# ConvFFN in three chunks of features, w_down by seven block products instead of eight, and pool tiles that wait only for the users of their own bytes

## The chip, the cores and the metric

The kernel runs as one program on one core of one Trainium2 chip. The metric is the device time of that core in microseconds (us); lower is better. A profiled execution of the same program gives the trace from which rows are read below. Engines are named as in the profile: PE is the matrix engine (PEld its weight loads), DVE the vector engine, ACT the scalar engine, POOL GpSimd, SP the engine that issues most DMAs. SBUF is the on-chip memory of 128 partitions; PSUM is the memory into which PE accumulates.

## The reference

One trunk layer is computed for 128 context tokens and 512 latent tokens (640 columns in all). The first part (adaptive norm, latent attention, a bidirectional state-space scan, gates, output projection) leaves a residual stream x of 1024 features. The change rewrites the last part, the ConvFFN:

```python
h2 = rmsnorm(x, lp['norm_ffn_g']) * (1 + sc2) + sh2
u = dwconv_centred(h2 @ lp['w_up'], lp['ffn_conv_w'], lp['ffn_conv_b'])
x = x + g2 * ((jax.nn.silu(u[..., :D_FF]) * u[..., D_FF:]) @ lp['w_down'])
y = rmsnorm(x, final_norm_g)
```

D_FF is 2816, so `w_up` is 1024 x 5632 and `w_down` 2816 x 1024. `dwconv_centred` is a depthwise convolution of width 3 along the tokens, for each request by itself.

## The kernel before

Data stand with features on partitions and the 640 tokens along the free axis; a tile of 128 features x 640 tokens is a "page" (2.5 KB a partition, 21 of them in the pool `pg`). Every matmul of weights is done to nearly full fp32 precision with three passes of the fp32r type: an operand is split into a high part (an ACT cast, L105) and a low part (a subtraction on POOL or DVE, L102), and `mm3` (L129) multiplies high by high, high by low and low by high. One 128 x 128 block of weights against 640 tokens is therefore six matmuls, three of 384 columns and three of 256 (`halves`), each with its own weight load.

Weights come by `wload`: an SP DMA into `raw` (4 buffers of 1024 columns), an ACT cast into `whi`, a POOL subtraction into `wlo` (2 buffers each), all in the pool `ws`, which lives through the whole kernel. So a whole tile of weights can be fetched and split while the tile before it is multiplied.

The ConvFFN follows the output projection. While the last three output tiles are finished, `h2_part` (L1142) makes the eight pages of h2 for the first 384 tokens and then for the other 256; it reads and overwrites the tiles `x1` of the pool `hold`. One `w_up` tile (`early`) and the first tiles of the loop run in between. Then 22 feature tiles are made (L1184): for each, two products with h2 into PSUM `big` (2 buffers), `conv` (ACT L453, four DVE instructions L455 and L458), SiLU (L1200), a multiply (L1201), and the split into the high and low part, 22 pairs of pages kept in `fl`, `fr` and `pg`. After that (L1209) each of the eight output tiles m runs over all 22 feature tiles, is added to x (`residual`, L1094) and squared for the last norm; the last tile does its two token parts one after the other, so that the norm and the output of the first (L1248) run beside the products of the second.

PE, ACT, DVE and POOL each execute their own list of instructions in order. Inside `tc.manual_schedule(engines=...)` the lists of the named engines are in the order of the program text; elsewhere a planner orders by its own estimates, the earlier in the text first among those that are ready. SP's DMAs are one such list too, so a DMA that waits for its buffer holds those behind it.

Tile pools are regions of SBUF that are opened and closed like a stack. Inside a pool each tag has its buffers in a row, tags in order of first use. When a pool is opened over the bytes of closed ones, its tiles wait for all users of those pools. The pools whose opening the prediction speaks of: `sp` (for the scan, L837, over `op2`, `sm` and `ar` of the attention's output), `yp` (L1043, over `sd` and `sp`), `hold` (L1106), `fl` and `fr` (L1181).

Of the kernel before, what the change touches and what calls it, by code (L numbers as in the profile page):

```python
# [10 lines left out]
F32 = mybir.dt.float32  # L11
F32R = mybir.dt.float32r
AF = mybir.ActivationFunctionType
ALU = mybir.AluOpType
# [45 lines left out]
RP = 2  # L60
LAG, F_T, F_V = 2, (1, 2), (1, 0, 1, 1, 1)
# [10 lines left out]
def trunk_kernel(ctx: ExitStack, tc: tile.TileContext, a: dict):  # L72
# [51 lines left out]
    def mm3(outs, hi, lo, rhs, first, last):  # L124

        plan = [(hi, rhs[0]), (hi, rhs[1]), (lo, rhs[0])]
        for i, (w, r) in enumerate(plan):
            for o, s in outs:
                PE.matmul(o, w, r[:, s], start=first and i == 0, stop=last and i == 2)  # L129
# [134 lines left out]
    tmp = sqp.enter_context(tc.tile_pool(name="tmp", bufs=3))  # L264
# [33 lines left out]
    gp = sqp.enter_context(tc.tile_pool(name="gp", bufs=16))  # L298
# [192 lines left out]
    op = ost.enter_context(tc.tile_pool(name="op", bufs=8, side="right"))  # L491
    awk = ExitStack()
    ap = awk.enter_context(tc.tile_pool(name="ap", bufs=1))
# [231 lines left out]
    sd = swk.enter_context(tc.tile_pool(name="sd", bufs=1))  # L725
    op2 = att.enter_context(tc.tile_pool(name="op2", bufs=16))
# [6 lines left out]
    xp = xst.enter_context(tc.tile_pool(name="xp", bufs=8, side="right"))  # L733

    sm = att.enter_context(tc.tile_pool(name="sm", bufs=1))
# [74 lines left out]
    ar = att.enter_context(tc.tile_pool(name="ar", bufs=1))  # L810
# [26 lines left out]
    sp = swk.enter_context(tc.tile_pool(name="sp", bufs=1))  # L837
# [205 lines left out]
    yp = ssd.enter_context(tc.tile_pool(name="yp", bufs=16))  # L1043
# [19 lines left out]
    mp = mst.enter_context(tc.tile_pool(name="mp", bufs=16, side="right"))  # L1063
    mer = []
    sxs = ExitStack()
    sx = sxs.enter_context(tc.tile_pool(name="sx", bufs=1, side="right"))
# [39 lines left out]
    hp_ = hold.enter_context(tc.tile_pool(name="hold", bufs=1))  # L1106
# [71 lines left out]

    sxs.close()
    mst.close()  # L1180
    fl = ctx.enter_context(tc.tile_pool(name="fl", bufs=28))  # L1181
    fr = ctx.enter_context(tc.tile_pool(name="fr", bufs=14, side="right"))
    act = []
    for i in range(NF):  # L1184
        us = []
        for j in range(2):
            if i == 1 and j == 0:
                p = early
# [20 lines left out]
    for m in range(8):  # L1209
# [5 lines left out]
        for k0 in range(0, NF, step):  # L1215
# [3 lines left out]
            if not last:  # L1219
                if k0 == 0:  # L1220
                    ps = big()
# [165 lines left out]
```

## Time and profile before

| what | us |
|---|---|
| median of three runs (1280.89 to 1287.76) | 1281.18 |
| the profiled execution, its own time | 1281.07 |
| its span in the trace | 1279.3 |
| PE busy within the span | 1217.2 |
| DVE, ACT, POOL busy | 727.4, 542.9, 496.7 |
| from the first products of the 22 feature tiles to the end | about 482 (797 to 1279) |

The busy time of PE counts overlapping matmuls once; it says that PE had work in flight, and only the number of matmuls in a stretch tells the pace. Of the other engines' times one reads whether they leave room beside PE in a given stage.

### The profile page before, as it was taken

How to read it: one execution, taken by the hardware profiler on the slowest of the kernel's cores; microseconds unless marked ns; L12 is line 12 of the kernel's file. 1: busy time of each engine (PE TensorE's matmuls, PEld its weight loads, DVE VectorE, ACT ScalarE, POOL GpSimd, SP SyncE). 2: the span in 40 equal slices, each digit the busy share in tenths (PEclk: the TensorE clock that was granted, in tenths of full speed). 3: DMA queues.
4: the chain of work that ended last, by engine and by line, in shares of the span. 5: the costliest groups of instructions: out<-in, count | busy, mean ns of one | idle time of the engine just before them, and what ended most of it. 6: DMA issues, size and time to landing. Idle time of an engine off the chain costs nothing. (4 is left out here: it accounts for less than half of the span.)

```text
span 1279.3 us, 20744 instructions
## 1 busy us (share of the span) xinstructions
PE 1217.2 (95%) x8361; PEld 1165.6 (91%) x8361; DVE 727.4 (57%) x1285; ACT 542.9 (42%) x943; POOL 496.7 (39%) x260
## 2 busy tenths in 40 slices
PE   8798999999998989899988998999999999999997
PEld 5698999999998987788888898999999999999996
DVE  4767656665558876866779989644444434300003
ACT  5455455545557425534763232533333333311220
POOL 3433021211213328845567365333333323334450
PEclk9999999999998999899989899999999999999999
DMA  8333221213128762123365674122212122242212
GB/s 330 127 102 102 80 68 54 80 68 108 54 95 284 250 230 93 63 81 108 103 219 186 219 246 133 42 82 67 82 67 83 67 82 68 84 151 75 75 46 83
DMA packets 53680, 148.23 MB, mean 116 GB/s; under 512 B 6224, under 2 KB 11792, under 8 KB 53584
## 3 DMA queue, kind: packets, MB, share of 16 engines
q1 hardware_dynamic: 51824, 144.80, 33.5%
q10 hardware_dynamic: 1760, 2.11, 0.6%
q8 instruction: 66, 1.08, 0.4%
q14 instruction: 30, 0.25, 0.1%
HBM read 124.01 MB, written 20.35 MB: 113 GB/s over the span
## 5 line engine op out<-in xcount | busy, mean ns | idle before, releaser
L129 PE MATMUL big<-pg,whi 128*128 128x384 f32 (+1 forms) x3752 | 726.8, 314 | 6.7 <-DVE pg L1083 4.4
L129 PEld LDWEIGHTS big<-pg,whi 128*128 128x128 f32 x3752 | 572.8, 190 | 19.9 <-issue 11.6
L102 POOL TENSOR_TENSOR wlo<-raw,whi 128x1024 fp32r<-128x1024 f32 (+1 forms) x128 | 319.8, 2499 | 593.0 <-ACT whi L105 587.4
L129 PE MATMUL big<-pg,wlo 128*128 128x384 f32 (+1 forms) x1876 | 436.6, 312 | 6.1 <-POOL wlo L102 6.0
L129 PEld LDWEIGHTS big<-pg,wlo 128*128 128x128 f32 x1876 | 292.5, 191 | 7.7 <-POOL wlo L102 7.1
L105 ACT CAST whi<-raw 128x1024 fp32r<-128x1024 f32 (+2 forms) x133 | 135.1, 1017 | 187.5 <-PE big L129 169.4
L455 DVE SCALAR_TENSOR_TENSOR st<-big,vec,st 128x127 f32<-128x127 f32 x68 | 37.0, 544 | 104.9 <-ACT st L453 104.9
L1094 DVE SCALAR_TENSOR_TENSOR pg<-big,mod,pg 128x128 f32<-128x128 f32 (+2 forms) x15 | 7.5, 542 | 124.8 <-PE big L129 124.8
L105 ACT CAST pg<-pg 128x640 fp32r<-128x640 f32 x46 | 33.0, 727 | 105.0 <-DVE pg L1201 67.1
L129 PE MATMUL sm<-pg,whi 128*128 128x384 f32 (+1 forms) x256 | 63.1, 327 | 4.1 <-ACT pg L105 2.5
L102 DVE TENSOR_TENSOR pg<-pg,pg 128x640 fp32r<-128x640 f32 x43 | 41.1, 963 | 23.8 <-ACT pg L105 23.8
L250 DVE SCALAR_TENSOR_TENSOR araw<-araw,crow 128x1024 f32<-128x1024 f32 x32 | 52.6, 1644 | 0.5
L129 PEld LDWEIGHTS sm<-pg,whi 128*128 128x128 f32 x256 | 46.0, 197 | 7.2 <-ACT pg L105 2.8
L455 DVE SCALAR_TENSOR_TENSOR pg<-big,vec,pg 128x127 f32<-128x127 f32 (+1 forms) x42 | 22.9, 546 | 51.3 <-ACT pg L453 51.3
L102 DVE TENSOR_TENSOR ptl<-sm,pth 128x512 fp32r<-128x512 f32 (+1 forms) x48 | 29.6, 620 | 35.0 <-ACT pth L600 35.0
L584 ACT ACTIVATE p<-sm,st 128x320 f32<-128x320 f32 x64 | 33.2, 524 | 37.6 <-DVE st L582 37.6
L581 DVE TENSOR_REDUCE st<-sm 128x1 f32<-128x320 f32 (+1 forms) x72 | 31.5, 462 | 26.5 <-PE sm L577 26.5
L250 DVE SCALAR_TENSOR_TENSOR junk<-araw,crow 128x1024 f32<-128x1024 f32 x32 | 45.7, 1428 | 0.0
L600 ACT CAST pth<-sm 128x512 fp32r<-128x512 f32 (+1 forms) x48 | 25.5, 533 | 43.7 <-PE sm L597 43.5
L129 PE MATMUL sm<-pg,wlo 128*128 128x384 f32 (+1 forms) x128 | 41.3, 323 | 0.3 <-POOL wlo L102 0.3
L458 DVE SCALAR_TENSOR_TENSOR st<-big,vec,st 128x127 f32<-128x127 f32 x68 | 37.2, 547 | 1.7
L1200 ACT ACTIVATE pg<-pg 128x640 f32<-128x640 f32 x22 | 16.3, 739 | 47.6 <-DVE pg L458 47.6
(294 smaller groups left out, 1737.3 us busy)
## 6 DMA issues: line engine op xcount, KB each, us to landing
raw<-w_up SPq DMA_DIRECT2D x44, 512.0 KB, 3.2
araw<-w_adar SPq DMA_DIRECT2D x32, 512.0 KB, 4.9
araw<-w_ada SPq DMA_DIRECT2D x16, 512.0 KB, 7.8
raw<-w_down SPq DMA_DIRECT2D x14, 512.0 KB, 3.5
raw<-w_xbc SPq DMA_DIRECT2D x12, 512.0 KB, 3.3
raw<-w_gm SPq DMA_DIRECT2D x8, 512.0 KB, 3.2
raw<-w_o_mla SPq DMA_DIRECT2D x8, 512.0 KB, 3.2
raw<-w_z SPq DMA_DIRECT2D x8, 512.0 KB, 4.5
```

Of the source, the lines that this page charges most:

```text
L102: return eng.tensor_tensor(out, x, f(hi), ALU.subtract)
L105: ACT.copy(hi, src)
L129: PE.matmul(o, w, r[:, s], start=first and i == 0, stop=last and i == 2)
L250: DVE.scalar_tensor_tensor(out, raw, 1.0, crow[r], ALU.mult, ALU.mult, accum_out=mod[:, j, r : r + 1])
L455: DVE.scalar_tensor_tensor(dst[:, lo_ + 1 : hi_], p[:, lo_ : hi_ - 1], vec[:, w : w + 1], dst[:, lo_ + 1 : hi_], ALU.mult, ALU.add)
L458: DVE.scalar_tensor_tensor(dst[:, lo_ : hi_ - 1], p[:, lo_ + 1 : hi_], vec[:, w + 2 : w + 3], dst[:, lo_ : hi_ - 1], ALU.mult, ALU.add)
L581: DVE.reduce_max(st[:, i : i + 1], sv, AX.X)
L584: ACT.activation(p[:, i * w : (i + 1) * w], sv, AF.Exp, bias=st[:, 2:3], scale=SCALE, accum_out=st[:, 4 + i : 5 + i])
L600: return ph, pl, ACT.copy(ph[:, :n], pt[:, :n]), sub(DVE, pl[:, :n], pt[:, :n], ph[:, :n])
L1094: ins = DVE.scalar_tensor_tensor(dst[:, lo_:hi_], ps[:, lo_ - cols.start : hi_ - cols.start], mod[:, gcol, r : r + 1], src[:, lo_:hi_], AL ...
L1200: ACT.activation(us[0], us[0], AF.Silu)
```

## The change

**Pools.** All pools but the constants, the pages, `ws` and PSUM get `reuse_waits="tile"`: a tile of such a pool waits for the users of the bytes that it covers, no longer for those of whole closed pools. `ws` is opened above `pg` and closed before the ConvFFN, where new pools `wf`, `kp` and `xs` take its place and that of the pools above it.

**Chunks.** The 22 feature tiles are worked in three chunks, 0 to 7, 8 to 15 and 16 to 21. After a chunk's tiles are made, their share of `w_down` is applied to all eight output tiles and added to x, which goes to DRAM and back between chunks.

**Seven products.** Within a chunk, feature tiles are taken in pairs (top, bottom), output tiles in pairs, and the tokens in two halves of 320, which makes a 2 x 2 by 2 x 2 block product. `blocks` makes the sums of activations that a seven-product scheme needs, `Pair.add` those of the weights, `Pair.product` runs the seven products with accumulation in three PSUM regions (`pa`, `pb`, `pc`), and `Pair.out` combines them into x on DVE. Weights are split in blocks of 512 columns (`operand`, tags `sh` and `sl`, 8 buffers each) rather than 1024. Between the chunks the two products of the next feature tile are run first. In the last chunk output tiles 0 to 3 are done so; 4 to 7 are done plainly, the first 384 tokens before and between the pairs, the other 256 after them.

The diff, cut to its core:

```diff
+CHUNKS = (0, 8, 16)
+LEAD, ON_DVE = 5, (4, 6)
...
-    ws = ctx.enter_context(tc.tile_pool(name="ws", bufs=2))
     pg = ctx.enter_context(tc.tile_pool(name="pg", bufs=21))
+    wss = ctx.enter_context(ExitStack())
+    ws = wss.enter_context(tc.tile_pool(name="ws", bufs=2))
...
-    sp = swk.enter_context(tc.tile_pool(name="sp", bufs=1))
+    sp = swk.enter_context(tc.tile_pool(name="sp", bufs=1, reuse_waits="tile"))
...
+    wss.close()
+    N2 = T // 2
+    lft, rgt = slice(0, N2), slice(N2, T)
+    ws = ctx.enter_context(tc.tile_pool(name="wf", bufs=2, reuse_waits="tile"))
+    kp = ctx.enter_context(tc.tile_pool(name="kp", bufs=24, reuse_waits="tile"))
+    xq = ctx.enter_context(tc.tile_pool(name="xs", bufs=4, reuse_waits="tile"))
...
+    def operand(x, n, eng):
+        hi, lo = (ws.tile([128, 512], F32R, tag=t, name=nm(t), bufs=8) for t in ("sh", "sl"))
+        h_, l_ = hi[:, 0:n], lo[:, 0:n]
+        if len(x.shape) == 3:
+            h_, l_ = (t.rearrange("p (i c) -> p i c", c=128) for t in (h_, l_))
+        split(h_, l_, x, eng)
+        return hi, lo
...
+    def blocks(i, top, bot):
+        ta = page()
+        DVE.tensor_tensor(ta[:, lft], top[:, rgt], top[:, lft], ALU.subtract)
+        DVE.tensor_tensor(ta[:, rgt], bot[:, rgt], ta[:, lft], ALU.subtract)
+        if i >= CHUNKS[-1]:
+            if i < NF - 1:
+                t = page(F32R, kp)
+                b12[i] = (t[:, lft], t[:, rgt])
+            else:
+                b12[i] = (half(), half())
+            split(*b12[i], top[:, rgt])
+        DVE.tensor_tensor(top[:, rgt], bot[:, rgt], top[:, rgt], ALU.subtract)
+        out = []
+        for t in (top, bot, ta):
+            out.append((page(F32R, kp), page(F32R, kp)))
+            split(*out[-1], t)
+        DVE.tensor_tensor(bot[:, rgt], bot[:, lft], ta[:, rgt], ALU.subtract)
+        out.append((half(), half()))
+        split(*out[-1], bot[:, rgt])
+        ops[i] = out
...
+    class Pair:
...
+        def add(self, n):
+            s = self.sums
+            x, y, op = {
+                1: lambda: (self.a21, self.a22, ALU.add),
+                2: lambda: (s[1], self.a11, ALU.subtract),
+                3: lambda: (self.a11, self.a21, ALU.subtract),
+                4: lambda: (self.a12, s[2], ALU.subtract),
+            }[n]()
+            s[n] = ws.tile([128, 512], F32, tag="sum", name=nm("sum"), bufs=4)[:, 0 : self.n * 128].rearrange("p (i c) -> p i c", c=128)
+            DVE.tensor_tensor(s[n], x, y, op)
+        def put(self, n):
+            s = self.sums
+            x = (lambda: self.a11, lambda: s[2], lambda: s[3], lambda: s[1], lambda: self.a12, lambda: s[4], lambda: self.a22)[n]()
+            self.w.append(operand(x, self.n * 128, DVE if n in ON_DVE else POOL))
+        def product(self, n):
+            if n == 0:
+                if self.last:
+                    self.pa, self.pb, self.pc, self.t = bank
+                else:
+                    ab = big()
+                    self.pa, self.pb, self.pc = ab[:, 0:N2], ab[:, 512 : 512 + N2], small()[:, 0:N2]
+            ps, b, cols, on = (
+                (self.pa, 0, lft, False), (self.pb, 2, rgt, False), (self.pc, 0, rgt, False), (self.pb, 2, lft, True),
+                (self.pa, 1, lft, True), (self.pb, 1, rgt, True), (self.pc, 3, lft, True),
+            )[n]
+            hi, lo = self.w[n]
+            for k in range(self.n):
+                s = slice(k * 128, (k + 1) * 128)
+                mm3([(ps, cols)], hi[:, s], lo[:, s], ops[self.k0 + 2 * k + 1][b], not on and k == 0, k == self.n - 1, on)
+        def temp(self):
+            return self.t if self.last else small()[:, 0:N2]
+        def to_x(self, j, ps, cols):
+            residual(self.x[j], ps, 40 + self.m + j, self.x[j], cols)
+        def out(self, n):
+            if n == 0:
+                self.p1 = part()
+                ACT.copy(self.p1, self.pa)
+            elif n == 1:
+                self.u2 = part()
+                DVE.tensor_tensor(self.u2, self.pb, self.p1, ALU.add)
+            elif n == 3:
+                u4, t = part(), self.temp()
+                DVE.tensor_tensor(u4, self.pb, self.p1, ALU.add)
+                DVE.tensor_tensor(t, self.pc, u4, ALU.add)
+                self.to_x(1, t, rgt)
+            elif n == 4:
+                self.to_x(0, self.pa, lft)
+            elif n == 5:
+                t = self.temp()
+                DVE.tensor_tensor(t, self.pb, self.p1, ALU.add)
+                self.to_x(0, t, rgt)
+            elif n == 6:
+                t = self.temp()
+                DVE.tensor_tensor(t, self.pc, self.u2, ALU.add)
+                self.to_x(1, t, lft)
+                if not self.last:
+                    for j in range(2):
+                        nc.sync.dma_start(xcd[self.c][self.m + j], self.x[j])
+    xcd = [[tc.dram_tile([128, T], F32, name=f"scr_xc{c}_{m}") for m in range(8)] for c in range(len(CHUNKS) - 1)]
+    def pairs(new, behind=(), between=None):
+        for t in range(7 * len(new) + 1):
+            g, s = divmod(t, 7)
+            if t:
+                new[(t - 1) // 7].out((t - 1) % 7)
+            if g == len(new):
+                break
+            now, nxt = new[g], new[g + 1] if g + 1 < len(new) else None
+            if s == 2:
+                if nxt:
+                    nxt.load_x()
+                if g + 2 < len(new):
+                    new[g + 2].load()
+            if nxt:
+                for n in ((1,), (2,), (), (3,), (), (4,), ())[s]:
+                    nxt.add(n)
+            n = s + LEAD - 7
+            if between and t == 7:
+                between()
+            if n < 0:
+                now.put(n + 7)
+            elif nxt:
+                if between and n == 0:
+                    behind[0]()
+                nxt.put(n)
+            elif n < len(behind) and not between:
+                behind[n]()
+            now.product(s)
...
+    made = {}
+    for c in range(len(CHUNKS) - 1):
+        first, nxt = CHUNKS[c], CHUNKS[c + 1]
+        for i in range(first + (c > 0), nxt):
+            for j in range(2):
+                u = made.pop((i, j), None) or Up(i, j)
+                if (i, j) != (1, 0):
+                    u.fetch()
+                if (i, j) == (nxt - 1, 1):
+                    ahead = [Up(nxt, 0), Up(nxt, 1)]
+                    for v in ahead:
+                        v.fetch()
+                    new = [Pair(c, m) for m in range(0, 8, 2)]
+                    new[0].load()
+                    ready(new[0])
+                    for n in range(LEAD - 1):
+                        new[0].put(n)
+                up_tile(u, early if (i, j) == (1, 0) else None)
+        with tc.manual_schedule(engines={PE.engine, ACT.engine, DVE.engine, POOL.engine}):
+            us[nxt, 0] = up_conv(nxt, 0, ahead[0].product())
+            silu(us[nxt, 0])
+            new[0].put(LEAD - 1)
+            new[0].load_x()
+            new[1].load()
+            us[nxt, 1] = up_conv(nxt, 1, ahead[1].product())
+            DVE.tensor_tensor(us[nxt, 0], us[nxt, 0], us.pop((nxt, 1)), ALU.mult)
+            nu = [Up(nxt + 1, j) for j in range(2)]
+            made = {(nxt + 1, j): nu[j] for j in range(2)}
+            behind = [lambda: (nu[0].load(), nu[0].put(0)), lambda: nu[0].put(1), lambda: (nu[1].load(), nu[1].put(0)), lambda: nu[1].put(1)]
+            pairs(new, behind)
...
+            if (i, j) == (NF - 1, 0):
+                new = [Pair(c, m) for m in (0, 2)]
+                new[0].load()
+                ready(new[0])
+                for n in range(LEAD):
+                    new[0].put(n)
...
+    def cut(i, c):
+        top, bot, *_ = ops[i | 1]
+        if i % 2:
+            return [(bot, c, slice(0, c.stop - c.start))]
+        out = []
+        if c.start < N2:
+            n = min(c.stop, N2) - c.start
+            out.append((top, slice(c.start, c.start + n), slice(0, n)))
+        if c.stop > N2:
+            s = max(c.start, N2)
+            out.append((b12[i | 1], slice(s - N2, c.stop - N2), slice(s - c.start, c.stop - c.start)))
+        return out
+    def plain(m, ps, c, ks):
+        for k in ks:
+            if k < NF - 1:
+                s = slice((k - k0) * 128, (k - k0 + 1) * 128)
+                w = wn[m]
+                s = slice((m - 4) * 128, (m - 3) * 128)
+                w = wlast
+            cs_ = cut(k, c)
+            plan = [(w[0], 0), (w[0], 1), (w[1], 0)]
+            for n, (w_, x) in enumerate(plan):
+                for b, src, o in cs_:
+                    PE.matmul(
+                        ps[:, o], w_[:, s], b[x][:, src], start=k == k0 + 1 and n == 0, stop=k == ks[-1] and n == 2,
+                        skip_group_check=True,
+                    )
...
+    ks = [k0 + 1, k0, *range(k0 + 2, NF)]
+    c0, c1 = PARTS
+    whole = slice(0, T)
+    with tc.manual_schedule(engines={PE.engine, ACT.engine, DVE.engine, POOL.engine}):
+        pn = [small()[:, 0:HALF] for _ in tiles]
+        for m, ps in zip(tiles, pn):
+            plain(m, ps, c0, ks[:-1])
+        ab, cd = big(), big()
+        bank = (ab[:, 0:N2], ab[:, 512 : 512 + N2], cd[:, 0:N2], cd[:, 512 : 512 + N2])
+        raw = rawtile()[:, 0:512]
+        nc.sync.dma_start(
+            raw.rearrange("p (m c) -> p m c", c=128), a["w_down"][4:8, :, (NF - 1) * 128 : NF * 128].rearrange("m p c -> p m c")
+        )
+        wlast = []
+        new[0].load_x()
+        new[1].load()
+        for m in tiles:
+            x2[m] = page()
+            nc.sync.dma_start(x2[m], xcd[-1][m])
+        def between():
+            x2[0], x2[1] = new[0].x
+            for m in (0, 1):
+                finished(m, whole, whole)
+            for m, ps in zip(tiles, pn):
+                plain(m, ps, c0, ks[-1:])
+                residual(x2[m], ps, 40 + m, x2[m], c0)
+                finished(m, c0, c0)
+            sqrt_table(acc)
+        pairs(new, [lambda: wlast.extend(operand(raw, 512, POOL))], between)
+        x2[2], x2[3] = new[1].x
+        for m in (2, 3):
+            finished(m, whole, c1)
+        last = [sqs[2], sqs[3]]
+    def scaled_out(rp, c):
         for m in range(8):
             g = vec[:, V_GFIN + m : V_GFIN + m + 1]
             DVE.scalar_tensor_tensor(x2[m][:, c], x2[m][:, c], g, rp, ALU.mult, ALU.mult)
             nc.sync.dma_start(a["out_y"][m][:, c], x2[m][:, c])
+    with tc.manual_schedule(engines={PE.engine}):
+        w1 = c1.stop - c1.start
+        ab, cd = big(), big()
+        for m, ps in zip(tiles, (ab[:, 0:w1], ab[:, 512 : 512 + w1], cd[:, 0:w1], cd[:, 512 : 512 + w1])):
+            plain(m, ps, c1, ks)
+            if m == 5:
+                ss = sumsq([acc, *last], c0)
+            if m == 6:
+                scaled_out(rstd_rows(ss, D, c0), c0)
+            residual(x2[m], ps, 40 + m, x2[m], c1)
+            finished(m, c1, c1 if m < 7 else None)
+        scaled_out(rstd_rows(sumsq([acc, sqs[7]], c1), D, c1), c1)
```

## Rows read from the trace of the kernel before

**Rows 1.** Page of the profile, its first line.

```profile
span 1279.3 us, 20744 instructions
```

**Rows 2.** Chain of work that ended last: start, time, engine, line.

```profile
822.16 425.27 PE big L129 x2892
```

**Rows 3.** Windows, the stretch of `w_down`: busy of PE, PEld, DVE, ACT, POOL; clock.

```profile
1010.00:1247.00 237.00, 237.00 (x1613) 237.00 (x1612) 50.88 (x88) 65.86 (x78) 92.03 (x44) 1.00 0.27 83
```

**Rows 4.** Timeline of PE, 128-column matmuls: start, busy time.

```profile
331.30 0.28 PE L129 MATMUL sm<-kh,ql 128*128 128x128 f32 x1
331.41 0.27 PE L577 MATMUL sm<-krh,qr 128*128 128x128 f32 x1
331.52 0.27 PE L577 MATMUL sm<-krl,qr 128*128 128x128 f32 x1
```

**Rows 5.** Timeline of DVE near 810, splitting `x1`.

```profile
809.70 0.42 DVE L102 TENSOR_TENSOR pg<-x,pg 128x256 fp32r<-128x256 f32 x1
```

**Rows 6.** Groups by form of PE, 797 to 811.4, matmuls of `big`.

```profile
L129 PE MATMUL big<-pg,whi 128*128 128x384 f32 x30 | 8.8, 349 | 0.0
L129 PE MATMUL big<-pg,wlo 128*128 128x384 f32 x14 | 4.7, 336 | 0.0
```

**Rows 7.** Windows, 811.4 to 822.16, columns as before.

```profile
811.40:822.16 10.76, 9.40 (x70) 8.62 (x70) 6.94 (x18) 6.31 (x11) 4.95 (x5) 1.00 0.01 2
```

**Rows 8.** Timeline, one feature tile from conv to split.

```profile
1097.69 0.88 ACT L453 ACTIVATE st<-big,vec 128x640 f32<-128x640 f32 x1
...
1100.82 0.82 DVE L1201 TENSOR_TENSOR pg<-pg,st 128x640 f32<-128x640 f32 x1
...
1101.67 0.73 ACT L105 CAST pg<-pg 128x640 fp32r<-128x640 f32 x1 [3.10 <-DVE pg L1201]
```

**Rows 9.** Groups by form of DVE, whole run: count, busy, mean ns.

```profile
L998 DVE TENSOR_TENSOR k<-k,k 128x512 f32<-128x512 f32 x20 | 28.5, 1424 | 12.4 <-POOL k L997 10.3 <-ACT k L988 2.1
...
L1010 DVE TENSOR_TENSOR k<-sm,pg 128x512 f32<-128x512 f32 x16 | 10.3, 683 | 1.2 <-PE sm L1008 1.2
...
L102 DVE TENSOR_TENSOR ql<-sm,qh 128x320 fp32r<-128x320 f32 x16 | 7.1, 484 | 9.5 <-ACT qh L105 9.5
L1094 DVE SCALAR_TENSOR_TENSOR x<-sm,mod,x 128x256 f32<-128x256 f32 x14 | 6.7, 476 | 1.6 <-PE sm L129 1.6
...
L1094 DVE SCALAR_TENSOR_TENSOR x<-sm,mod,x 128x128 f32<-128x128 f32 x8 | 2.8, 344 | 3.3 <-PE sm L129 3.3
```

**Rows 10.** Groups by form of ACT, whole run.

```profile
L105 ACT CAST qh<-sm 128x320 fp32r<-128x320 f32 x16 | 6.0, 429 | 3.4 <-PE sm L129 3.4
...
L1200 ACT ACT_TABLE_LOAD x1 | 1.3, 1283 | 0.0
```

**Rows 11.** Timeline of PE, its longest wait there in brackets.

```profile
410.12 0.72 PE L767 MATMUL sm<-dA,cons 128*128 128x80 f32 x2 [5.53 <-DVE dA L764]
```

**Rows 12.** Windows behind two waits, clock in the column after POOL.

```profile
410.00:414.00 4.00, 3.88 (x16) 3.88 (x17) 4.00 (x9) 2.45 (x4) 0.00 (x0) 0.54 0.74 242
478.50:482.00 3.50, 3.50 (x17) 3.50 (x16) 1.51 (x3) 2.70 (x6) 1.46 (x2) 0.51 1.01 316
```

**Rows 13.** Timeline of DVE, the scaled output near the end.

```profile
1263.94 4.29 DVE L1248 SCALAR_TENSOR_TENSOR pg<-pg,vec,sm 128x384 f32<-128x384 f32 x8 [1.01 <-PE sm L175]
```

**Rows 14.** Timeline around the loads of `bc`; SPq issues DMAs.

```profile
471.94 0.23 DVE L251 TENSOR_SCALAR mod<-mod,vec 128x2 f32<-128x2 f32 x1
471.98 1.75 SPq L846 DMA_DIRECT2D bc<-scr_xbc  x4
...
476.28 0.33 PE L857 MATMUL sm<-cons,bc 128*128 128x128 f32 x1 [0.54 <-ACT bc L847]
...
478.16 0.33 PE L857 MATMUL sm<-cons,bc 128*128 128x128 f32 x1 [1.55 <-ACT bc L847]
```

**Rows 15.** Timeline of DVE, one of the products for `ys`.

```profile
654.30 0.87 DVE L1056 SCALAR_TENSOR_TENSOR pg<-pg,vec,pg 128x640 fp32r<-128x640 f32 x1
```

**Rows 16.** Groups by form of POOL, 822 to 1010.

```profile
L102 POOL TENSOR_TENSOR wlo<-raw,whi 128x1024 fp32r<-128x1024 f32 x27 | 64.7, 2397 | 122.8 <-ACT whi L105 122.8
```

More of the change, by code (lines that the diff above doesn't have):

```diff
@@ L128, in mm3 @@
             for o, s in outs:
-                PE.matmul(o, w, r[:, s], start=first and i == 0, stop=last and i == 2)
+                PE.matmul(o, w, r[:, s], start=first and i == 0, stop=last and i == 2, skip_group_check=on)
     def halves(ps):
@@ new lines, in operand, with __init__, load, fetch @@
+    def operand(x, n, eng):
[5 more added lines that the diff above has]
+        return hi, lo
+    class Up:
+        def __init__(self, i, j):
+            self.i, self.j, self.w = i, j, []
+        def load(self):
+            self.raw = rawtile()
+            nc.sync.dma_start(self.raw, a["w_up"][2 * self.i + self.j])
+        def put(self, n):
+            self.w.append(operand(self.raw[:, 512 * n : 512 * n + 512], 512, POOL))
+        def fetch(self):
+            if not self.w:
+                self.load()
+                self.put(0)
+                self.put(1)
+        def product(self):
+            ps = big()
+            for outs in [[o] for o in halves(ps)] if self.i == 0 else [halves(ps)]:
+                for k in range(8):
+                    (hi, lo), s = self.w[k // 4], slice(k % 4 * 128, k % 4 * 128 + 128)
+                    mm3(outs, hi[:, s], lo[:, s], h2[k], k == 0, k == 7)
+            return mid(ps)
@@ new lines, in ready, with up_tile, up_join @@
+    def ready(pair):
+        for n in (1, 2, 3, 4):
+            pair.add(n)
+    us = {}
+    def up_tile(u, p=None):
+        i, j = u.i, u.j
+        if p is None:
+            u.fetch()
+            p = u.product()
+        us[i, j] = up_conv(i, j, p)
+        if j:
+            up_join(i)
+            if i % 2:
+                blocks(i, us.pop((i - 1, 0)), us.pop((i, 0)))
+    def up_join(i):
+        silu(us[i, 0])
+        DVE.tensor_tensor(us[i, 0], us[i, 0], us.pop((i, 1)), ALU.mult)
@@ new lines, in trunk_kernel @@
+    c = len(CHUNKS) - 1
+    k0 = CHUNKS[c]
+    nk = NF - k0
+    tiles = range(4, 8)
+    wn = {}
+    for i in range(k0 + 1, NF):
+        for j in range(2):
+            up_tile(made.pop((i, j), None) or Up(i, j))
+            if i == NF - 2:
+                for m in tiles[2 * j : 2 * j + 2]:
+                    raw = rawtile()[:, 0 : (nk - 1) * 128]
+                    nc.sync.dma_start(raw, a["w_down"][m][:, k0 * 128 : (NF - 1) * 128])
+                    hi, lo = ((page(F32R, xq if j else kp)) for _ in range(2))
+                    split(hi, lo, raw, POOL)
+                    wn[m] = (hi, lo)
+            if (i, j) == (NF - 1, 0):
[4 more added lines that the diff above has]
+                    new[0].put(n)
```

131 lines of the change are left out of this document (56 added, 75 removed).

## Prediction

> **What bounds the kernel now.** I read the page's head first for the span: 1279.3 us of the execution's 1281.07, so 1.8 us lie around it [rows 1]. Then the chain of work that ended last: its longest step is matmuls of `mm3` alone, from 822.16 for 425.27 us [rows 2]. Then windows for the pace inside it: while `w_down` runs, PE is busy all 237.00 us with 1613 matmuls, 0.1469 us each [rows 3]. They are half of 384 and half of 256 columns, 320 in the mean, so columns set the time: 0.46 us per 1000 columns, or 0.175 for 384, 0.1175 for 256 and 0.147 for 320. Matmuls of 128 columns start 0.11 us apart, where columns alone would give 0.06 [rows 4]; short ones have a floor. The reader is to see that here only fewer columns or fewer waits of PE count; DVE, ACT and POOL are busy 51, 66 and 92 of 237 us in it. Ahead of 797 PE has its waits, and there the pools' edges matter.
>
> **The change part by part**, against 1281.07.
>
> *Columns of `w_down`.* Before: 8 x 22 x 6 = 1056 matmuls x 0.1469 = 155.1 us. After, products by seven: 2 chunks x 4 pairs x 7 x 4 x 3 = 672, and 2 pairs x 7 x 3 x 3 = 126, so 798 x 0.147 = 117.3. The four plain tiles need each 9 x 0.175 for odd features, 9 x (0.147 + 0.11) for even ones, whose 384 columns come as 320 + 64, and 18 x 0.1175: 6.0, in all 24.0. Sum 141.3: **-13.8**. The 36 pieces of 64 columns are bounded by the floor (taken, since 128 columns stand there already) and by their columns (0.03), which makes -16.7.
> The Trainium skill ("TensorE: Matmul & The Clock Gate", section "LDWEIGHTS (loading the stationary operand)") has the weight load take time by the columns of the weights, 107 ns for 128, however few columns then stream through; the rows agree (0.11). By it the pieces cost an estimated 2.8 us above their columns; if loads hid behind the neighbour, the sum would be 2.9 lower.
>
> *Start of the ConvFFN.* The new pool `wf` lies where `ws` and the pools above it were: `raw` on its old bytes, the high parts on `whi` and `wlo`, the low parts from 32 KB on, over `dg` and the tiles `x1`. Those are read until 809.70 and later [rows 5], so the first low part of `w_up` can't be written before. In the kernel before, 44 matmuls of `big` with 384 columns fill PE between 797 and 811.4 [rows 6]: 44 x 0.175 = 7.7 us of cover that comes later instead. Of this, 10.76 - 9.40 = 1.36 us of idle between 811.4 and 822.16 [rows 7] would be filled, and high parts may run ahead. Bounds 0 and 7.7; I take **+4.5**.
>
> *First pair of chunks 1 and 2.* PE comes from the last `w_up` product with only that product's successor as cover. DVE then owes one conv (0.88 on ACT and 2.25 to the multiply), the multiply 0.82 [rows 8], two weight sums and one split of 512 columns, 0.69 each (by the 0.683 of L1010, [rows 9]), and `u2`, 0.48 (the same width took 0.484, [rows 9]): 6.5, with handovers 6.8. The fourth product overwrites what `u2` reads, and three products last 3 x 12 x 0.147 = 5.3. So 1.5 each, **+3**; bounds 0 (POOL and ACT far ahead) and 4.6.
>
> *Last chunk, plain tile 4.* Its k = 20 needs `blocks(21)`: from the conv's start to the cast took 1097.69 to 1101.67 = 3.98 [rows 8]; two dependent subtractions of 320 (0.48 each) come between, then the cast 0.73 [rows 8] and a subtraction of 640, 0.8. High part at 5.7, low at 6.5 after the product. PE has k = 17, 16, 18, 19 of tile 4 first: 6 x 0.175 + 6 x 0.257 = 2.6, and 0.26 between. **+3.9**, by 3.3 to 5.2. The other plain tiles stand behind it on PE.
>
> *Last chunk, second pair.* `between` puts four residuals (0.48 + 0.34, [rows 9]) and a split of the sixth operand's kind ahead of `u2` on DVE, and that split waits for ACT: six squares (two of 640, four of 384 columns, some 3.5 by the casts), a table load of 1.28 and two casts of 0.43 [rows 10]. With the first pair's last combination ahead, about 9.3 until `u2`; PE has 4 x 3 x 0.175 = 2.1 and three products of 9, 3.97. Gap 3.2, some tenths on top: **+3.5** (2.5 to 5).
>
> *Clock after a gap.* Behind a wait of 5.53 us [rows 11] the granted clock was 0.54 for the next 4 us, about the 1.2 GHz level, and 0.51 from 478.5 to 482 [rows 12]; half speed for 3.5 us costs 1.7. One of the two waits above will be long enough: **+1.7** (0 to 5).
>
> *The end.* Eight L1248 instructions of 384 columns took 4.29 us at 1263.94 [rows 13] beside 42 matmuls. Now they lie on DVE ahead of the last tile's residual, and PE has one tile, 18 x 0.1175 = 2.1, beside them: **+2.2**.
>
> *Pools.* `bc` is fetched at 471.98, just after the last DVE user of `ar` at 471.94; PE then waits 0.54 + 1.55 for it [rows 14] and runs at 0.51 from 478.5 to 482 [rows 12]: 2.1 + 1.7 = 3.8. The tiles of `yp` are an edge too; three L1056 of 0.87 [rows 15] could go earlier, 2.6. With both, -6.4, taken as **-6.5**. Bounds: -13.8, if the wait of 5.53 and its slow clock (1.8) go as well; +3.8, if the planner, seeing other edges, makes one more such gap.
>
> *At nothing.* `blocks` costs DVE some 4.9 us per two feature tiles (5 x 0.48, 3 x 0.83), with their convs and multiplies 15.3, beside four `w_up` products of 48 x 0.147 = 7 us each; without that cover the 4.9 would count 11 times. x goes to DRAM and back, 32 pages of 0.33 MB more; the DMAs' share was 0.27 at 83 GB/s [rows 3], so nothing. If an x load waits on SP for its buffer, the weight loads behind it wait too; the splits made ahead, a product's worth, cover that.
>
> Sum: -13.8 + 4.5 + 3 + 3.9 + 3.5 + 1.7 + 2.2 - 6.5 = -1.5, so 1279.5. The profiled execution is 0.1 below the median of the runs, so nothing is to be added.
>
> **The rivals.**
> *Faster.* The waits at the chunks' edges are covered: the split products have slack elsewhere, because one `w_up` product lasts 7 us. Then 4.5 + 3 fall away, and with a third more of what the pools could give (2.4): 1269.6, say 1270. For it speaks that DVE is idle most of the last 240 us; against it, that the order is fixed by hand there.
>
> *Slower: DVE becomes the bound of the pairs, through POOL.* A subtraction with two operands in SBUF (L998) took 1.424 us for 512 columns beside a busy POOL, and with one in PSUM (L1010) 0.683 [rows 9]. Four weight sums and two splits a pair are of that kind, and POOL splits five operands a pair beside them, 1.2 each (half of 2.397, [rows 16]). DVE owes a pair 6 x 0.69 + 5 x 0.48 + about 1.1 + 2 x (0.35 + 0.41) = 9.1 against PE's 84 x 0.147 = 12.35. With each of the six at 1.42 it is 13.5: 1.15 late in 8 pairs; in the last chunk 12.8 against 9.26, 3.5 in 2 pairs: +16.3 in place of 3 + 3.5. That is 1289.3. It decides from a mean wait of (12.35 - 9.1)/6 = 0.54 us per instruction. For it speaks L998; against it, that the two together hold the lock only 4.1 + 6 = 10.1 of 12.35.
> The Trainium skill ("SBUF — State Buffer", section "Who interferes with whom") says that DVE and GpSimd share a pair of SBUF ports under an exclusive lock, so that the one that comes second stands still. The trace agrees with 1.424 against 0.683; by the rule the wait would be up to a whole POOL instruction, 1.2.
>
> *The pools' edges move nothing*, since DMAs or DVE hold those places anyway: 1279.5 + 6.5 = 1286. That is the change not doing this part of what it says.
>
> **How the numbers follow.** Forecast, 1274 to 1285: 0.38. Faster rival: 0.32. DVE as bound: 0.15. Pools without effect: 0.15. About 0.5%, 6.4 us, is what a measurement of this kernel can tell from no change: 1274.8 to 1287.6. Nearly all of the forecast lies inside, with a small part below; the faster rival is outside for the most part; DVE as bound is outside on the other side, the pools' rival partly, with the outer bounds of the clock term: faster 0.36, same 0.42, slower 0.22. The range takes the faster rival to 1264 (the pieces of 64 columns at 2.9 less, more of the pools) and the DVE one to 1293 (a second clock gap and the rest of the bounds); the likeliest case's own is 1274 to 1285.
>
> **What would show it.** In the profile after: `w_down` takes 798 matmuls of 320 columns at 0.147; starts 0.11 apart for the pieces of 64. Idle PE before `ahead`'s successors behind L102 or the cast (chunks' edges), before k = 20, and before the fourth product of the second pair, each near its term; granted clock near half behind the longest. The `bc` wait near 476 to 478 is gone. The last L1248 of 384 columns end after the last matmul. Wrong would make it: the seven-product pairs at a pace far from 12.35 us, long DVE instructions beside POOL's, a new wait ahead of 797, or none of the four waits in the last 90 us.

## The result and the profile after

The changed kernel took 1317.12 us (median of four, 1316.40 to 1321.52) against 1281.04 for the kernel before: ratio 1.0282, 95% interval 1.0235 to 1.0329. It is slower by 36 us, where 1279.5 was forecast, and outside the range of 1264 to 1293. The profiled execution took 1321.52 us; its span is 40.5 us longer than that of before [rows 1].

```profile
span 1319.8 us, 21251 instructions
...
PE 1220.4 (92%) x8289; PEld 1157.4 (88%) x8289; DVE 862.4 (65%) x1519; ACT 582.2 (44%) x1073; POOL 524.8 (40%) x336
```

PE is busy 3.2 us longer than before, though it has fewer columns; the rest is waiting, and in places a granted clock of 0.50, the lower of its two levels (1.2 GHz).

The pairs. First a window of one steady pair (columns as in [rows 3]):

```profile
951.00:966.00 15.00, 13.13 (x86) 12.34 (x85) 9.72 (x18) 4.37 (x8) 6.36 (x6) 1.00 0.47 158
```

86 matmuls in 15 us; at the pace of [rows 3] it would be 102. The timeline of such a pair shows where the time is. The lines are products 4 to 6, counted from 0, then 0 and 1 of the next pair, with the readers that PE waits for:

```profile
1148.72 0.49 DVE L1348 TENSOR_TENSOR o<-big,o 128x320 f32<-128x320 f32 x1 [1.44 <-PE big L134]
...
1149.27 0.55 PE L134 MATMUL big<-pg,sh 128*128 128x320 f32 x2 [0.58 <-DVE o L1348]
...
1151.33 0.68 DVE L1099 SCALAR_TENSOR_TENSOR pg<-big,mod,pg 128x128 f32<-128x128 f32 x2 [0.99 <-PE big L134]
...
1152.06 0.56 PE L134 MATMUL big<-pg,sh 128*128 128x320 f32 x2 [0.77 <-DVE pg L1099]
...
1153.93 0.45 PE L134 MATMUL sm<-hf,sh 128*128 128x320 f32 x2
...
1155.69 0.45 PE L134 MATMUL big<-pg,sh 128*128 128x320 f32 x2
...
1157.64 0.42 ACT L1342 COPY o<-big 128x320 f32<-128x320 f32 x1 [4.31 <-PE big L134]
...
1158.12 0.57 PE L134 MATMUL big<-pg,sh 128*128 128x320 f32 x2 [0.52 <-ACT o L1342]
```

Product 4 writes `pa`, and starts when DVE's L1348 has read `pb`. Product 5 writes `pb`, and starts when L1099 has read `pa`. Product 1 writes `pb`, and starts when ACT's copy (L1342) has read `pa`. Products 6 and 0 follow without a wait: they write `pc`, and the other `ab`. Each time PE waits for the reader of what it has just finished, in a region that the next product doesn't touch. `pa` and `pb` are two banks of one tile `ab`. In the trace each of these waits ends at a semaphore of that reader. Products 4, 5 and 1 start 0.75, 0.93 and 0.68 us late (a start less the one before and its columns' time), and the second matmul of each another 0.1. The list of waits, for the two pair loops (total, times, longest):

```profile
PE big L134 <- DVE pg L1099: 4.6, 6, 0.8
PE big L134 <- ACT o L1342: 4.1, 8, 0.5
PE big L134 <- DVE o L1348: 3.5, 6, 0.6
PE big L134 <- DVE o L1345: 2.9, 2, 1.5
```

The last line is the wait for `u2` that was forecast at 1.5 for each first pair; it is 1.63 in the starts.

The start of the ConvFFN, beside [rows 7, 12]; the fourth line is the kernel before:

```profile
785.00:800.00 15.00, 11.88 (x55) 9.46 (x54) 11.94 (x30) 5.57 (x12) 5.12 (x6) 0.79 0.45 146
800.00:812.00 12.00, 8.97 (x28) 6.36 (x27) 7.68 (x20) 4.57 (x13) 3.55 (x5) 0.50 0.33 126
812.00:822.30 10.30, 9.95 (x52) 9.57 (x51) 0.00 (x0) 4.07 (x8) 10.30 (x9) 0.74 0.41 153
...
800.00:812.00 12.00, 11.78 (x71) 11.02 (x71) 8.12 (x22) 4.15 (x10) 3.50 (x4) 1.00 0.06 22
```

```profile
796.73 1.96 SPq L1221 DMA_DIRECT2D raw<-w_up  x4
...
802.02 0.73 ACT L1158 CAST pg<-x 128x256 fp32r<-128x256 f32 x2 [2.02 <-DVE x L1156]
...
810.44 0.37 ACT L1176 COPY pg<-sm 128x256 f32<-128x256 f32 x1 [1.70 <-PE sm L134]
...
810.70 1.66 ACT L110 CAST sh<-raw 128x512 fp32r<-128x512 f32 x3
811.38 0.50 PEld L134 LDWEIGHTS big<-pg,sh 128*128 128x128 f32 x2 [1.27 <-ACT sh L110]
```

The w_up loads go out at 796.73, behind the last stores of x1, and ACT casts them behind the last copy of h2's stage, from 810.70 on. They had landed between 801.4 and 805.5, and ACT stood idle for 0.7 to 2.0 us at a time between 800 and 810.4: the casts stand late in ACT's list, and the loads don't hold them. The first `big` product with 384 columns starts at 811.38, where the kernel before had run 44 [rows 6]. PE has little between 790 and 811, and from 794 on its granted clock is 0.50, so that the products of h2 and the output projection's rest are slowed as well; before, PE was busy 11.78 of the same 12 us at 1.00.

The last chunk: the wait before k = 20 and the clock behind it, then the chain before the second pair's product 1, then the scaled output ([rows 13]):

```profile
1244.48 1.98 ACT L110 CAST pg<-pg 128x640 fp32r<-128x640 f32 x3 [4.03 <-DVE pg L1263]
...
1245.26 0.64 PE L1501 MATMUL sm<-pg,pg 128*128 128x320 f32 x1 [3.13 <-ACT pg L110]
```

```profile
1245.00:1250.00 5.00, 4.57 (x18) 4.38 (x18) 3.19 (x5) 1.92 (x4) 0.00 (x0) 0.50 0.00 0
```

```profile
1274.76 5.85 POOL L1515 TENSOR_TENSOR pg<-pg,pg 128x640 f32<-128x640 f32 x5 [7.24 <-ACT pg L1513]
...
1277.09 1.28 ACT L187 ACT_TABLE_LOAD   x1
1280.64 0.20 ACT L187 ACTIVATE dummy<-pg 128x1 f32<-128x1 f32 x1 [2.27 <-POOL pg L1515]
1280.75 0.49 ACT L110 CAST sh<-sum 128x384 fp32r<-128x384 f32 x1
1281.15 0.42 ACT L1342 COPY o<-big 128x320 f32<-128x320 f32 x1
...
1281.62 0.50 PEld L134 LDWEIGHTS big<-pg,sh 128*128 128x128 f32 x2 [5.82 <-ACT o L1342]
...
1304.04 4.29 DVE L1558 SCALAR_TENSOR_TENSOR pg<-pg,vec,sm 128x384 f32<-128x384 f32 x8 [0.16 <-PE sm L180]
```

k = 20 is 3.3 us late; behind it 5 us run at 0.50. Before the second pair, POOL's five additions (5.85 us) end at 1280.6; the load of the square-root table is done 2.3 us before, but the small instruction that triggers it (`dummy`) reads `acc` and waits for them. The cast and the copy of `pa` stand behind it on ACT, and product 1 waits for the copy: 5.7 us late. The forecast had `u2` in this place.

### The profile page after: what moved, and what is told of

Its sections match the earlier page's. It is cut to its first block, busy times and chain, and to the rows that moved or that the text cites. A ratio compares the mean times of both kernels' runs of the same rounds, so it can differ in the third digit from the quotient of the medians.

```text
span 1319.8 us, 21251 instructions
## 1 busy us (share of the span) xinstructions
PE 1220.4 (92%) x8289; PEld 1157.4 (88%) x8289; DVE 862.4 (65%) x1519; ACT 582.2 (44%) x1073; POOL 524.8 (40%) x336
## 5 line engine op out<-in xcount | busy, mean ns | idle before, releaser
L134 PE MATMUL big<-pg,sh 128*128 128x384 f32 (+2 forms) x1768 | 353.1, 313 | 26.6 <-ACT o L1342 10.2
L134 PE MATMUL big<-pg,whi 128*128 128x384 f32 (+1 forms) x1760 | 347.6, 319 | 4.6 <-DVE pg L1088 2.8
L134 PEld LDWEIGHTS big<-pg,sh 128*128 128x128 f32 x1768 | 274.2, 189 | 34.9 <-ACT o L1342 12.8
L107 POOL TENSOR_TENSOR wlo<-raw,whi 128x1024 fp32r<-128x1024 f32 (+1 forms) x64 | 169.6, 2653 | 322.9 <-ACT whi L110 319.6
L134 PEld LDWEIGHTS big<-pg,whi 128*128 128x128 f32 x1760 | 271.3, 192 | 18.0 <-issue 11.2
L134 PE MATMUL big<-pg,sl 128*128 128x384 f32 (+2 forms) x884 | 221.3, 310 | 0.3 <-POOL sl L107 0.3
L134 PE MATMUL big<-pg,wlo 128*128 128x384 f32 (+1 forms) x880 | 205.8, 314 | 5.5 <-POOL wlo L107 5.5
L107 POOL TENSOR_TENSOR sl<-raw,sh 128x512 fp32r<-128x512 f32 (+1 forms) x97 | 129.7, 1345 | 189.7 <-ACT sh L110 181.2
L134 PEld LDWEIGHTS big<-pg,sl 128*128 128x128 f32 x884 | 144.2, 189 | 0.9 <-POOL sl L107 0.9
L134 PEld LDWEIGHTS big<-pg,wlo 128*128 128x128 f32 x880 | 138.3, 192 | 6.8 <-POOL wlo L107 6.3
```

What stands on the lines that cost most here:

```text
L107: return eng.tensor_tensor(out, x, f(hi), ALU.subtract)
```

## The experiments

Two theories on the pairs. A: PE's writes to one bank of a two-bank tile wait for the readers of the other. B: the products wait because ACT and DVE read the results too slowly, wherever they lie. For the start of the ConvFFN, first the forecast's reason (low parts over `x1`), then the order in which loads and casts for the new pool come.

Each ratio is to the kernel before on the same chip. Stages are also compared within the profiles, since the part ahead of the ConvFFN, which most edits don't touch, ends up to 8.7 us apart in them.

**pa apart.**

```diff
-                    ab = big()
-                    self.pa, self.pb, self.pc = ab[:, 0:N2], ab[:, 512 : 512 + N2], small()[:, 0:N2]
+                    self.pa, self.pb, self.pc = big()[:, 0:N2], small()[:, 0:N2], small()[:, 0:N2]
```

> Theory A (PE's writes to one region of a two-bank PSUM tile wait for the readers of its other region): with the pair's regions pa and pb in tiles of their own in chunks 1 and 2, the three waits of 0.68, 0.75 and 0.93 us in each of the 8 pairs vanish, 18.9 us, so about 1298 against 1317 for the changed kernel; the waits in the last chunk stay. Theory B (the pair's products wait because ACT and DVE read the results too slowly, whatever tile they are in): the waits stay or move to other products, within 3 us of 1317.

1310.50 us (1305.55 to 1314.09), ratio 1.0245 (1.0213 to 1.0277). All three waits are gone from the two loops; what is left there is the wait for `u2`:

```profile
PE sm L134 <- DVE o L1344: 4.5, 2, 2.3
```

```profile
947.90:951.50 3.60, 3.60 (x15) 3.60 (x16) 1.91 (x2) 1.76 (x3) 2.27 (x3) 0.57 0.49 146
```

That is 0.8 longer than before, since PE comes sooner, and PE's clock is 0.57 for 3.6 us behind it. The loops take 53.3 us each, where they took 59.95 without the next tile's products in them: 13.2 us less. Expected were 18.9, by a count of three waits in every pair; the last pair of each chunk had only one, because products of the next tile run there between its own, so the waits were 17.5 us, and 4 came back at `u2`. Theory A holds; the size was 4 us off. The median fell by 6.6 only: in the two profiles the part up to the norm behind the scan, which the edit doesn't touch, ends 4.5 later here, and the part from there to the end takes 11.9 less.

**pb and pc together.**

```diff
-                    ab = big()
-                    self.pa, self.pb, self.pc = ab[:, 0:N2], ab[:, 512 : 512 + N2], small()[:, 0:N2]
+                    bc = big()
+                    self.pa, self.pb, self.pc = small()[:, 0:N2], bc[:, 0:N2], bc[:, 512 : 512 + N2]
```

> Now pb and pc share a two-bank tile and pa is apart. Theory A: the waits move to where a product follows a reader of its neighbour: before the third product (behind the read of pb for u2) and before the seventh (behind the read of pb for the upper right block), some 0.75 us each; none before the second, fifth and sixth. 1.5 in place of 2.36 a pair, so 1308 to 1312. Theory B: the waits stay before the second, fifth and sixth product, 1317.

1322.56 us, ratio 1.0345 (1.0328 to 1.0362). The waits moved to where theory A puts them, before the third product (behind L1345, the read of `pb`) and before the seventh (behind L1355), and PE waits for no reader of ACT or DVE before the others. First the first pair's wait for `u2`, then two of the steady ones:

```profile
940.42 0.56 PE L134 MATMUL big<-pg,sh 128*128 128x320 f32 x2 [3.99 <-DVE o L1345]
...
949.95 0.53 PE L134 MATMUL big<-hf,sh 128*128 128x320 f32 x2 [0.68 <-DVE sm L1355]
...
956.14 0.53 PE L134 MATMUL big<-pg,sh 128*128 128x320 f32 x2 [0.68 <-DVE o L1345]
```

The time is not the expected one: the first pair's third product now waits 4.0 us for `u2`, which the fourth did for 1.5, and the granted clock is 0.63 from 940.4 to 944. The loops take 60.5 us each, where the changed kernel took 59.95.

**The first operands clear of x1.**

```diff
-        hi, lo = (ws.tile([128, 512], F32R, tag=t, name=nm(t), bufs=8) for t in ("sh", "sl"))
+        two = "" if opn[0] % 8 < 4 else "2"
+        opn[0] += 1
+        hi, lo = (ws.tile([128, 512], F32R, tag=t + two, name=nm(t), bufs=4) for t in ("sh", "sl"))
```

> The first four operands of the ConvFFN lie wholly over the old whi and wlo (two sets of four buffers instead of one of eight), clear of the x1 tiles. Theory A (the first w_up products are late because their low parts lie over x1): some 44 matmuls of 384 columns come back as cover before the last h2 parts, the first conv moves 8 us earlier, 1309. Rival: the first products wait for something else (the casts on ACT, the weights' loads), and the time stays at 1317.

1321.37 us, ratio 1.0334 (1.0318 to 1.0349): no gain. The first casts of w_up still start right behind the last copy, at 809.07, and the loads are as late. That the low parts lie over `x1` is not what holds the start; the theory fell.

**The pools alone**: the kernel before with `reuse_waits="tile"` at the fourteen pools of the diff, and nothing else.

> Kernel before with only the pools' waits by tile. By the shifts between the two traces ahead of the ConvFFN it should be 4 to 6 us faster than before, 1276, with the wait for bc near 476 gone and the 5.5 us wait at 404 to 410 still there. Rival: the gain seen there came from other places' order, and this alone is within 2 us of 1281.

1275.32 us (ten runs), ratio 0.9972 (0.9955 to 0.9989): 3.6 us faster. The wait for `bc` is 1.33 long instead of 0.54 and 1.55, and the clock behind it full:

```profile
474.63 0.33 PE L857 MATMUL sm<-cons,bc 128*128 128x128 f32 x1 [1.33 <-ACT bc L847]
```

```profile
476.00:480.00 4.00, 4.00 (x35) 4.00 (x34) 3.00 (x7) 4.00 (x9) 1.61 (x2) 1.00 0.91 274
```

The first conv comes at 814.2 instead of 818.6. The wait of 5.53 [rows 11] stays.

**The first w_up tiles through the old pool**, on top of pa apart:

```diff
+    for j in range(2):
+        whi, wlo = wload(a["w_up"][j], 1024)
+        ps = big()
...
+        pre[0, j] = mid(ps)
     wss.close()
```

> On the kernel with pa apart: the first feature tile's two w_up tiles are loaded and split through the old pool and multiplied ahead of the new pools' opening. Theory A (what the new pool does at its opening puts loads and casts of w_up behind all of h2, so PE stands between 790 and 812 and its clock falls to half): the products run between the h2 parts again, the clock stays at full, and the ConvFFN's first conv comes some 9 us earlier, at about 814 to 818 instead of 822 to 827; the whole time 9 less than with pa apart alone. Rival (it is the waits' new order of h2 itself): no change.

1307.21 us (two runs), ratio 1.0196 (1.0149 to 1.0244). The clock is 1.00 from 800 to 812, and the first conv comes at 817.9. Counted from the last matmul of the norm behind the scan, at 666.6 here and at 670.0 with pa apart alone, that is 5.8 earlier. But PE then stands for the next tile's weights:

```profile
820.77 0.88 ACT L458 ACTIVATE st<-big,vec 128x640 f32<-128x640 f32 x1 [1.14 <-PE big L134]
...
821.67 1.28 ACT L1256 ACT_TABLE_LOAD   x1
...
822.97 1.36 ACT L1256 ACTIVATE pg<-pg 128x640 f32<-128x640 f32 x2
...
824.24 2.16 ACT L110 CAST sh<-raw 128x512 fp32r<-128x512 f32 x4
...
824.89 1.44 PE L134 MATMUL big<-pg,sh 128*128 128x384 f32 x4 [4.16 <-ACT sh L110]
```

Their casts come behind both convs, a table load and the SiLU on ACT. They had landed by 812.2. From the norm to the first pair 1.5 us are left of the gain (268.7 against 270.2), where 9 were expected. What was put into the new pool is late again, one tile later, by the order of ACT's list. Whether these casts also had to wait for the old pool's weights, whose bytes the new pool takes over, no run separates.

**Single banks in the last chunk, weight sums behind u2**, on top of pa apart:

```diff
-        pn = [small()[:, 0:HALF] for _ in tiles]
+        ab, cd = big(), big()
+        pn = [ab[:, 0:HALF], cd[:, 0:HALF], ab[:, 512 : 512 + HALF], cd[:, 512 : 512 + HALF]]
...
-        bank = (ab[:, 0:N2], ab[:, 512 : 512 + N2], cd[:, 0:N2], cd[:, 512 : 512 + N2])
+        bank = [small()[:, 0:N2] for _ in range(4)]
...
-                for n in ((1,), (2,), (), (3,), (), (4,), ())[s]:
+                for n in ((), (), (1, 2), (3,), (), (4,), ())[s]:
```

> On the kernel with pa apart: in the last chunk the pairs' four regions lie in single banks and the plain tiles' sums share the two-bank tiles; weight sums of the next pair are made after u2. Theory A: the waits in the last chunk's pairs before the second, fifth and sixth products (0.67 to 0.93 each) and before the first plain tiles behind them (0.75 each) vanish, 6 to 7 us; the wait for u2 of 2.42 in chunks 1 and 2 falls below 0.3 and the half clock behind it stays away, 3.9 each. Together 13 less than with pa apart alone. Theory B: the last chunk's waits stay at those products since they wait for ACT and DVE themselves.

1290.22 us (seven runs), ratio 1.0075 (1.0054 to 1.0096). From the last `w_up` product to the end it takes 69.6 us instead of 81.2, 11.6 less where 6 to 7 were expected: the 5.2 us before the second pair's product 1 went too, since that product writes `pb` and no longer waits for the copy of `pa`. The loops are 2.9 shorter each; `u2` is still 1.0 late. Two plain tiles now share a tile, and their wait (L1099) is new; the second line is the second pair's wait for `u2`:

```profile
1249.64 0.62 PE L1500 MATMUL big<-pg,sh 128*128 128x384 f32 x2 [1.50 <-DVE pg L1099]
...
1258.38 0.53 PE L134 MATMUL sm<-pg,sh 128*128 128x320 f32 x2 [1.54 <-DVE o L1344]
```

**k = 20 last, the table behind the pairs**, on top of pa apart:

```diff
-            plain(m, ps, c0, ks[:-1])
+            plain(m, ps, c0, ks[:-2])
+        for m, ps in zip(tiles, pn):
+            plain(m, ps, c0, ks[-2:-1])
...
-            sqrt_table(acc)
+        sqrt_table(sqs[3])
```

> On the kernel with pa apart: k = 20 of the plain tiles comes after the other k of all four, and the square-root table is loaded after the second pair. Expected: the wait of 3.3 us before k = 20 and the half clock behind it (3 us) vanish; the wait of 5.2 to 5.7 before the second product of the second pair loses the POOL additions that the table's load waited for, and falls to about 2.2. Together 9 less. Rival: the wait before k = 20 moves to k = 21 or to the first pair's operands.

1296.38 us (two runs), ratio 1.0112 (1.0061 to 1.0163). From the last `w_up` product to the end: 68.8 instead of 81.2, 12.4 less where 9 were expected. No wait before k = 20 or 21 and none on POOL's sums; the wait before product 1 is 1.95.

**All together**, with the first squares behind `u2` and the scaled output in two halves:

> All of these together, the squares of the first tiles put behind u2 of the second pair, and the scaled output in two halves around the last residual. If the terms add up: 1310 - 9 - 13 - 9 - 2 - 2 = 1275, a few us below the kernel before. Rival: waits that stood behind others come out, and it stays above 1281.

1282.11 us (ten runs, 1275.94 to 1285.73), ratio 1.0000 (0.9979 to 1.0022). The median is 7 above the sum of the terms, and the rival's 1281 is passed: waits that stood behind others came out. The 4.3 us behind the first feature tile stay, and 2.5 between plain tiles.

**The remaining waits**, on top of that (fetches ahead in the text, plain products ahead of their residuals, the multiply behind `u2`):

> All of these, and: the fetch of the second and third feature tile's w_up stands ahead of the first conv in the text; the four plain products before the second pair come first and their four residuals behind them; the multiply between the two w_up products of the next chunk comes after u2. Expected against the kernel with all of these before: the wait of 4.3 us behind the first feature tile and the half clock behind it go (6), the wait of 2.5 us between plain tiles goes, u2's wait of 1.0 falls by 0.8 in two chunks: 10 less, about 1272, 0.5 to 0.8% below the kernel before. Rival: the loads of these tiles are late themselves, and the first wait stays.

1275.68 us (six runs), ratio 0.9963 (0.9948 to 0.9978): by the ratios 4.7 us less than the version before, where 10 were expected. The pieces of 64 columns cost what the forecast took for them: the 96 matmuls of the plain tiles ahead of the pairs take 14.28 us, 0.84 of it a wait, where columns alone give 10.58 and 36 pieces at 0.11 give 13.5. The starts are not 0.11 apart, though: in the changed kernel's trace the next matmul starts 0.03 us after such a piece and the one after it 0.23 later, 0.26 for both. The pair loops have no wait above 0.2 and take 49.28 us each, 12.32 a pair, where 12.35 was forecast. The first wait stays, as the rival said, but not for its reason: the loads landed between 801.5 and 806.5, and ACT casts them from 818.2 on, behind convs, table load and SiLU. The text's order didn't change ACT's.

```profile
PE big L134 <- ACT sh L110: 4.2, 1, 4.2
PE big L134 <- DVE pg L463: 2.0, 2, 1.1
```

**The third product through the old pool too:**

```diff
+    for j in range(2):
+        us[0, j] = stage() if j else page()
+        conv(us[0, j], pre[0, j], V_FW + 3 * j, V_FB + j)
+    whi, wlo = wload(a["w_up"][3], 1024)
...
     wss.close()
```

> The third w_up product (second half of the second feature tile) too is loaded, split and multiplied through the old pool, and the first two convs stand ahead of it. Theory A (what stands behind the opening of the new pool is put late in the orders of SP and ACT: the first casts of w_up come behind the convs, the table load and the SiLU): the 4.3 us wait behind the first feature tile is covered by this product's 7 us, the clock stays at full from 812 to 825, 5 us less than with the version before, about 1270. Rival: the wait comes one product later, since the loads are late by more than a product; then about the same time.

1273.59 us (ten runs, 1271.78 to 1277.13), ratio 0.9955 (0.9938 to 0.9973), the fastest here. The clock is full up to 825; the wait of 4.3 is now two of 1.7, one for a conv on DVE and one for a cast. From the norm to the first pair: 265.5, 4.7 less than with pa apart alone. In the kernel before as many matmuls of `w_up` (17 products of 48, 816 in all) would be done 822.16 + (816 - 96) x 0.1469 - 667.9 = 260.0 after the norm. By the interval it can't be told from the version before it, nor from the pools alone. So no run shows that the 13.8 us of columns bring more than the pools' waits do by themselves.

## Why the prediction was wrong

The sum against the profiled execution, by its own terms:

| term | forecast | measured |
|---|---|---|
| columns of w_down | -13.8 | -13.8 |
| start of the ConvFFN | +4.5 | +11 |
| first pair, `u2` | +3 | +3.3 |
| products waiting for the neighbour's reader, pair loops | 0 | +17.5 |
| the same in the last chunk | 0 | +7.8 |
| a conv late on DVE, ahead of a chunk's last feature tile | 0 | +1.9 |
| k = 20 | +3.9 | +3.3 |
| second pair | +3.5 | +5.7 |
| half clock behind these | +1.7 | +4.5 |
| the end | +2.2 | +4.1 |
| pools | -6.5 | -4.5 |
| sum | -1.5 | +40.8 (span: +40.5) |

Measured are late starts of matmuls (a start less the one before and the columns' time) and slow stretches in the profile; the convs' line and the end's have no experiment of their own. The pools' term is the shift of the first conv with the pools alone, and the start's is what is then missing at 822 (4.5 + 6.5). The end is 3.1 from the last product on and 1.0 of the norm's sums among the products. The convs' line is of what the forecast put at nothing: in the trace the conv stands behind the first pair's four weight sums and the work of `blocks` on DVE.

**The step that failed** is the pace of the pairs: "798 x 0.147 = 117.3", with waits of PE looked for only where a product overwrites what a reader still needs (`u2`). The columns were right, and 12.35 a pair is reached when the regions lie in tiles of their own and `u2` comes in time (12.32). In the change as made a product also waits for the readers of the other bank of its tile; moving `pb` beside `pc` moved the waits as this says. That is 25.3 of the 42 us between forecast and profile, and in the last chunk it also set the 5.7 us: the second pair's product 1 writes `pb`, and waited for a copy of `pa` that stood behind POOL's sums.

**The start** had its mechanism half right and its size wrong. The cover of 44 products was lost, as forecast. Its bound of 7.7 counted their columns alone; PE's sparse work then ran at 0.50, and the lead of 4.5 from the pools became a lag: at 822 the kernel before had done 96 matmuls of `w_up` in `big` (the 44 of [rows 6] and 52 of the 70 in [rows 7]), the changed one 52 at 822.3, so it was behind by 44 x 0.147 = 6.5. The reason given, low parts over `x1`, is refuted. What the runs show is that the casts for the new pool stand late in ACT's list, behind loads that have long landed, and that the same products through the old pool don't. Why the planner puts them there was not shown, and 5.5 us of the loss (265.5 against 260.0) are not recovered by any version here.

**k = 20 and the second pair** were late as forecast; in the second the chain ran through the table's read of `acc` and the copy of `pa`, where the forecast had the split and `u2`.

**The pools** gave 3.6 us by themselves, where 6.5 was taken: the `bc` wait is shorter by 0.8 and the clock behind it full, as said. The rival in which the pools' edges move nothing is out, by an interval of 1.4 to 5.8 us.

**The rivals.** The faster rival had the waits at the chunks' edges covered; `u2`, k = 20 and the second pair were all late, so it is out. The slower rival named DVE as the bound of the pairs. DVE is busy 9.72 of 15 us there, and its mean wait is too short: the 28 weight sums took 28.4 us and the 16 splits 11.0 in the two loops, 0.90 each, 0.2 above the 0.69 of one alone, where 0.54 would decide. No rival named the wait that decided.

```profile
L107 DVE TENSOR_TENSOR sl<-raw,sh 128x512 fp32r<-128x512 f32 x16 | 11.0, 687 | 6.4 <-ACT sh L110 5.8
L1308 DVE TENSOR_TENSOR sum<-raw,raw 128x512 f32<-128x512 f32 x7 | 10.7, 1522 | 0.0
...
L1308 DVE TENSOR_TENSOR sum<-raw 128x512 f32<-128x512 f32 x7 | 7.0, 996 | 1.1 <-DMA raw<-w_down 1.1
...
L1308 DVE TENSOR_TENSOR sum<-raw,sum 128x512 f32<-128x512 f32 x7 | 5.9, 838 | 0.0
...
L1308 DVE TENSOR_TENSOR sum<-sum,raw 128x512 f32<-128x512 f32 x7 | 4.8, 691 | 0.5
```

The Trainium skill ("SBUF — State Buffer", section "Who interferes with whom") lets the second of DVE and GpSimd stand still on their shared ports. The trace agrees: the same sum, `sum<-raw,raw` of 512 columns, took 0.69 us with POOL idle and 1.67 us when POOL had begun a split 0.16 us before it, and then ended 0.55 us behind POOL's.

```profile
899.65 0.69 DVE L1308 TENSOR_TENSOR sum<-raw,raw 128x512 f32<-128x512 f32 x1
...
1145.45 1.28 POOL L107 TENSOR_TENSOR sl<-sum,sh 128x512 fp32r<-128x512 f32 x1
...
1145.61 1.67 DVE L1308 TENSOR_TENSOR sum<-raw,raw 128x512 f32<-128x512 f32 x1
```

In the pairs it can have cost no more than part of the wait for `u2`, which fell from 2.4 to 1.0 us when the weight sums were put behind `u2`.

## What to carry to other kernels

Before counting a product at its columns, ask for each PSUM tile who else reads it: two accumulators that are drained at different times should not be two banks of one tile, even where no byte is shared. In an order written by hand, follow one step further what a reader on the path waits for; the operand of the small instruction that loads a table is enough to tie ACT to POOL (the wait before product 1 fell from 5.2 to 1.95 when it was moved). And when a pool is closed and opened anew in front of a stage, look at what the first loads and casts of that stage ran beside before: losing such cover costs its columns and the clock.

## Not expected of the hardware

That PE's clock stood at 0.50 from 800 to 812 in a stretch of short waits, the longest 1.6 us, in which PE shows 8.97 of 12 us busy; and that a single wait of 2.3 us was followed by 3.6 us at 0.57, where the forecast had expected that of its longest wait alone. In the changed kernel the 1.5 us wait for `u2` was followed by a full clock (1.00 from 943 to 947).
